# The six buffers of converted weights begin 128 bytes lower in each SBUF partition

## The chip, the cores and the metric

The kernel runs on one core of one Trainium2 chip. The metric is the device time of one execution in microseconds (us). A profile is one execution recorded by the hardware profiler; its engines are PE (TensorE's matmuls), PEld (TensorE's weight loads), DVE (VectorE), ACT (ScalarE), POOL (GpSimd) and SP (the queue that issues most DMAs).

## The reference

One layer of a decoder trunk on 256 tokens of width 2048, all in float32. Shortened to what matters here:

```python
mod = silu(c) @ w_ada + b_ada                     # 2048 -> 6 * 2048: shifts, gains, gates
h = rms_norm(x, norm_mix) * (1 + sc1) + sh1
proj = h @ w_in                                   # 2048 -> three groups of heads
mixed = concat(retention(proj), rwkv7(proj), moba_attention(proj))
x = x + g1 * (mixed @ w_out)                      # 2048 -> 2048
h = rms_norm(x, norm_ffn) * (1 + sc2) + sh2
u = causal_conv3(h @ w_ffn_up) + conv_b           # 2048 -> 2 * 5632
val, gate = split(u)
x = x + g2 * ((silu(gate) * val) @ w_ffn_down)    # 5632 -> 2048
return rms_norm(x, norm_final)
```

The four large products (w_in, w_out, w_ffn_up, w_ffn_down) are nearly all of the arithmetic.

## The kernel before

**How a large product is computed.** Activations lie feature-major: 128 features on the partitions, 256 tokens along the free dimension. A weight matrix comes as blocks of 128 x 128; such a block is the stationary operand of a matmul and a 128 x 256 activation tile is the moving one. For accuracy every value is split in two parts of type fp32r, hi (the rounded value) and lo (what the rounding left), and each block of the product takes three matmuls into one PSUM tile: hi weights with hi activations (line 1192), hi weights with lo activations (1193), lo weights with hi activations (1194). Each of the three loads its own weights, so 3,200 blocks make 9,600 pairs of weight load and matmul. The names of the activation tiles tell the stage: hhi and hlo are the normalised input of w_in and of w_ffn_up, mxhi and mxlo that of w_out, xghi and xglo an early input for the first part of w_ffn_up, ghi and glo the input of w_ffn_down.

**How weights arrive.** SP loads raw weights in tiles of 128 x 2048 float32 (raw). For each half of such a tile `convert_until` (line 448) lets ACT round it into a buffer hi of 8 blocks (line 458) and DVE subtract to get lo (line 459). There are CONVB = 3 buffers hi and 3 buffers lo, used in turn, 4,096 bytes per partition each; block j of a buffer begins 512 j bytes into it. Conversion runs AHEAD = 2 buffers ahead of the matmuls. The order of the instructions on each engine is that in which the Python code issues them; the outer loop (line 1166) takes one converted buffer after another, 8 blocks each, then evacuates finished tiles and runs some steps of the attention-like tasks, whose smaller matmuls lie between those of the large products.

**Where tiles lie.** Pools are laid out one after the other in each partition, and inside a pool in the order of first use: const, arena (30 tiles of 4,096 bytes), stream (three raw buffers of 8,192 bytes, a pad, the three hi, the three lo), small (narrow vectors of the norms, the tile rs_mix / acc / rs_ffn, a pad, more small tiles), and behind them a region that is reused from stage to stage. The start addresses in the built program, per partition:

| tiles | bytes each | first start | start modulo 512 |
|---|---|---|---|
| arena: x, hhi, hlo, mxhi, mxlo, most of ghi and glo, late raw tiles | 4,096 | 31,232 | 0 |
| stream: raw | 8,192 | 154,112 | 0 |
| stream: hi and lo, six buffers | 4,096 | 179,008 | 320 |
| small: narrow vectors of 8 bytes | 8 | 203,584 | 320 to 416 |
| small: rs_mix, acc, rs_ffn | 1,024 | 203,712 | 448 |
| small: xn, nsq | 1,024 | 204,800 | 0 |
| last region, tail: xghi, and the second glo | 4,224 | 207,232 | 384 |
| last region, tail: the first glo | 4,224 | 211,456 | 0 |
| last region, tail: the first ghi | 4,224 | 215,680 | 128 |
| last region, tail: xglo, and the second ghi | 4,224 | 219,904 | 256 |

The tiles inside an activation buffer are 1,024 bytes apart (1,032 for xghi and xglo, which have 258 columns), so the moving operand of nearly all large matmuls begins at a multiple of 512 bytes, and every weight block at 320 modulo 512. The exceptions are the 192 matmuls with xghi and xglo and, in w_ffn_down, the first 24 matmuls of each of the 16 output tiles, which take the tail's ghi and glo. Two pads have a size that the code states: the stream pad at line 348 and SMALL_PAD at line 1061.

Of the kernel before, what the change touches and what calls it, by code (L numbers as in the profile page):

```python
# [8 lines left out]
F32 = mybir.dt.float32  # L9
# [156 lines left out]
WAITS = (7, 20, 28)  # L166
TASKS = 5

CONST_PAD, SMALL_PAD = 32, 16

LEAD = ((116, 0), (145, 8), (152, 6), (164, 4), (172, 3), (186, 1))

# [1 line left out]
def trunk(tc, A):  # L174
# [5 lines left out]
    def pool(name, bufs, **kw):  # L180
        return ctx.enter_context(tc.tile_pool(name=name, bufs=bufs, **kw))
# [3 lines left out]
    stream = pool("stream", 1)  # L185
# [159 lines left out]

    pump()

    stream.tile([128, 80], F32, name="pad")


    silu_c = const.tile([128, 16], F32, name="silu_c")
# [928 lines left out]
```

## Time and profile before

| | |
|---|---|
| median of 3 runs | 1285.11 us (1283.68 to 1285.34) |
| the profiled execution | 1284.61 us, of which the span from first to last instruction is 1282.8 us |
| granted TensorE clock, mean | 0.987 |
| PE busy | 1242.3 us (97%), 10,524 matmuls |
| DVE, ACT, POOL busy | 1031.6 us (80%), 650.6 us (51%), 39.9 us (3%) |
| bytes moved | 320.56 MB, mean 250 GB/s |

Matmuls overlap in the array: each stands in the trace with some 0.28 us although the next one starts about 0.11 us later. So the busy time of PE tells only whether PE ever stood still; how fast a run of matmuls goes is read from the distance between two starts, or from a stretch's length and the number of matmuls in it (two of which had begun before the stretch).

### The profile page before, as it was taken

How to read it: one execution, taken by the hardware profiler on the slowest of the kernel's cores; microseconds unless marked ns; L12 is line 12 of the kernel's file. 1: busy time of each engine (PE TensorE's matmuls, PEld its weight loads, DVE VectorE, ACT ScalarE, POOL GpSimd, SP SyncE). 2: the span in 40 equal slices, each digit the busy share in tenths (PEclk: the TensorE clock that was granted, in tenths of full speed). 3: DMA queues.
4: the chain of work that ended last, by engine and by line, in shares of the span. 5: the costliest groups of instructions: out<-in, count | busy, mean ns of one | idle time of the engine just before them, and what ended most of it. 6: DMA issues, size and time to landing. Idle time of an engine off the chain costs nothing.

```text
span 1282.8 us, 25320 instructions
## 1 busy us (share of the span) xinstructions
PE 1242.3 (97%) x10524; PEld 1222.0 (95%) x10524; DVE 1031.6 (80%) x1606; ACT 650.6 (51%) x1043; POOL 39.9 (3%) x41
## 2 busy tenths in 40 slices
PE   5899999999999999999999999999999999999996
PEld 4799999999998999999999999999999999999995
DVE  7988989989988478999896999899866766666444
ACT  4455444665435333566555656666555544444441
POOL 0000000000000000500000000000000000000000
PEclk7999999999999999999999999999999999999998
DMA  9999987786636459867985566565655677777551
GB/s 388 349 360 344 341 311 268 290 294 209 232 104 235 155 204 363 319 233 259 350 307 200 197 213 208 184 225 194 220 205 198 230 263 254 285 254 281 207 197 66
DMA packets 49939, 320.56 MB, mean 250 GB/s; under 512 B 5536, under 2 KB 6048, under 8 KB 15776
## 3 DMA queue, kind: packets, MB, share of 16 engines
q1 hardware_dynamic: 48528, 315.10, 67.8%
q0 software_dynamic: 1008, 3.67, 0.8%
q8 instruction: 82, 1.34, 0.4%
q14 instruction: 33, 0.27, 0.1%
q10 hardware_dynamic: 288, 0.17, 0.0%
HBM read 316.83 MB, written 2.10 MB: 249 GB/s over the span
## 4 chain that ended last, share of the span: by engine, by line
PE 89%; DVE 7%; issue 2%; ACT 1%; DMA 0%; POOL 0%; DVEq 0%; ACTq 0%; POOLq 0%
PE mm L1192 26%; PE mm L1194 26%; PE mm L1193 26%; DVE raw L413 2%; DVE lo L459 2%; PE pair L1194 1%; PE pair L1192 1%; PE pair L1193 1%; PE xx L778 1%; PE u L915 1%; PE sp L923 1%; PE sp L937 1%; PE akv L788 1%; PE yps L917 0%; ACT hi L458 0%
## 5 line engine op out<-in xcount | busy, mean ns | idle before, releaser
L459 DVE TENSOR_TENSOR lo<-raw,hi 128x1024 fp32r<-128x1024 f32 x400 | 488.4, 1224 | 161.0 <-ACT hi L458 158.2
L458 ACT CAST hi<-raw 128x1024 fp32r<-128x1024 f32 x400 | 418.7, 1049 | 391.7 <-PE mm L1193 333.0
L1192 PE MATMUL mm<-hhi,hi 128*128 128x256 f32 x2016 | 560.2, 278 | 0.2
L1194 PE MATMUL mm<-hhi,lo 128*128 128x256 f32 x2016 | 559.4, 278 | 0.7 <-DVE lo L459 0.7
L1193 PE MATMUL mm<-hlo,hi 128*128 128x256 f32 x2016 | 559.5, 278 | 0.0
L1194 PEld LDWEIGHTS mm<-hhi,lo 128*128 128x128 f32 x2016 | 379.2, 188 | 1.7 <-DVE lo L459 1.3
L1192 PEld LDWEIGHTS mm<-hhi,hi 128*128 128x128 f32 x2016 | 379.1, 188 | 1.3 <-issue 0.3
L1193 PEld LDWEIGHTS mm<-hlo,hi 128*128 128x128 f32 x2016 | 378.8, 188 | 0.3
L413 DVE SCALAR_TENSOR_TENSOR raw<-raw,cb 128x2048 f32<-128x2048 f32 x96 | 221.3, 2305 | 10.4 <-DMA raw<-w_ada 9.6
L1192 PE MATMUL mm<-ghi,hi 128*128 128x256 f32 x704 | 194.8, 277 | 0.0
L1193 PE MATMUL mm<-glo,hi 128*128 128x256 f32 x704 | 194.8, 277 | 0.0
L1194 PE MATMUL mm<-ghi,lo 128*128 128x256 f32 x704 | 194.8, 277 | 0.0
L1192 PEld LDWEIGHTS mm<-ghi,hi 128*128 128x128 f32 x704 | 132.2, 188 | 0.0
L1194 PEld LDWEIGHTS mm<-ghi,lo 128*128 128x128 f32 x704 | 132.2, 188 | 0.0
L1193 PEld LDWEIGHTS mm<-glo,hi 128*128 128x128 f32 x704 | 132.2, 188 | 0.0
L1192 PE MATMUL mm<-mxhi,hi 128*128 128x256 f32 x256 | 73.9, 289 | 1.3 <-DVE x L1032 1.3
L1194 PE MATMUL mm<-mxhi,lo 128*128 128x256 f32 x256 | 72.1, 282 | 0.5 <-DVE lo L459 0.5
L1193 PE MATMUL mm<-mxlo,hi 128*128 128x256 f32 x256 | 72.3, 283 | 0.0
L1046 POOL TENSOR_TENSOR acc<-acc,nsq 128x256 f32<-128x256 f32 x28 | 34.0, 1213 | 808.4 <-ACT nsq L1045 808.2
L1192 PE MATMUL pair<-hhi,hi 128*128 128x256 f32 x160 | 45.0, 294 | 7.6 <-ACT hi L458 5.6
L1192 PEld LDWEIGHTS mm<-mxhi,hi 128*128 128x128 f32 x256 | 48.3, 188 | 3.2 <-DVE x L1032 1.2
L1194 PEld LDWEIGHTS mm<-mxhi,lo 128*128 128x128 f32 x256 | 48.5, 189 | 0.6 <-DVE lo L459 0.6
(292 smaller groups left out, 1301.5 us busy)
## 6 DMA issues: line engine op xcount, KB each, us to landing
raw<-w_ada SPq DMA_DIRECT2D x96, 1024.0 KB, 5.7
raw<-w_up SPq DMA_DIRECT2D x67, 1024.0 KB, 4.8
raw<-w_in SPq DMA_DIRECT2D x52, 1024.0 KB, 6.6
raw<-w_down SPq DMA_DIRECT2D x44, 1024.0 KB, 4.9
raw<-w_up SPq DMA_DIRECT2D x42, 512.0 KB, 8.1
raw<-w_out SPq DMA_DIRECT2D x18, 512.0 KB, 9.1
raw<-w_out SPq DMA_DIRECT2D x7, 1024.0 KB, 5.0
x<-xT SPq DMA_DIRECT2D x4, 512.0 KB, 5.4
```

Of the source, the lines that this page charges most:

```text
L413: V.scalar_tensor_tensor(raw, raw, 1.0, cb, op0=OP.mult, op1=OP.mult, accum_out=m)
L458: S.copy(flat(hi), src)
L459: V.tensor_tensor(flat(lo), src, flat(hi).bitcast(F32), op=OP.subtract)
L778: PE.matmul(ps[:, T * i:T * i + 128], L[pb, f, sl], At[pb, f, sl], start=True, stop=True)
L788: PE.matmul(ps[:, 128 * i + 64 * e:128 * i + 64 * e + 64], xv[:, e, 128 * i:128 * i + 128], vT[:, h, 64 * hd:64 * hd + 64], start=True, st ...
L915: PE.matmul(ups[pb, 128 * f:128 * f + 128], M1[:, f, ts], sb[:, f], start=True, stop=True)
L923: PE.matmul(sp[:, fs], kT[pb, h, fs], vT[pb, h, fs], start=(f == 0), stop=False, skip_group_check=True)
L937: PE.matmul(sp[:, fs], bT[pb, h, fs], U[pb, h, fs], start=False, stop=True, skip_group_check=True)
L1046: (V if t == NF - 1 else G).tensor_tensor(norm["acc"], norm["acc"], sq, op=OP.add)
L1192: PE.matmul(ps, whi[:, j], hi, start=first and not (two and t % 2), stop=False, skip_group_check=two)
L1193: PE.matmul(ps, whi[:, j], lo, start=False, stop=False, skip_group_check=two)
L1194: PE.matmul(ps, wlo[:, j], hi, start=False, stop=last, skip_group_check=two)
```

## The change

Two pads of one column count change, the one by -32 float32 columns (128 bytes), the other by +32.

```diff
-CONST_PAD, SMALL_PAD = 32, 16
+CONST_PAD, SMALL_PAD = 32, 48
...
-    stream.tile([128, 80], F32, name="pad")
+    stream.tile([128, 48], F32, name="pad")
```

By this the six buffers hi and lo begin 128 bytes lower, at 192 modulo 512 in place of 320. The narrow 8-byte vectors and the tile rs_mix / acc / rs_ffn behind them move down with them (the tile from 448 to 320). The larger pad in small takes up the 128 bytes, so xn, nsq and all that follows stay where they were; so do const, arena and the raw buffers. Every instruction on every engine, its order and its waits are the same as before.

## Rows read from the trace of the kernel before

**Rows 1.** The page: engine busy time, and the granted clock in 40 slices
```profile
PE 1242.3 (97%) x10524; PEld 1222.0 (95%) x10524; DVE 1031.6 (80%) x1606; ACT 650.6 (51%) x1043; POOL 39.9 (3%) x41
...
PEclk7999999999999999999999999999999999999998
```

**Rows 2.** The page's costliest groups: out<-in, count, busy us, mean ns
```profile
L1192 PE MATMUL mm<-hhi,hi 128*128 128x256 f32 x2016 | 560.2, 278 | 0.2
...
L1192 PE MATMUL mm<-ghi,hi 128*128 128x256 f32 x704 | 194.8, 277 | 0.0
...
L1192 PE MATMUL mm<-mxhi,hi 128*128 128x256 f32 x256 | 73.9, 289 | 1.3 <-DVE x L1032 1.3
...
L1192 PE MATMUL pair<-hhi,hi 128*128 128x256 f32 x160 | 45.0, 294 | 7.6 <-ACT hi L458 5.6
```

**Rows 3.** Stretches of PE: from:to, length, PE busy (matmuls), granted clock, DMA share, GB/s
```profile
140.00:194.00 54.00, 54.00 (x461) 1.00 0.88 334
216.00:229.00 13.00, 13.00 (x117) 1.00 0.84 313
...
570.00:1027.00 457.00, 457.00 (x4035) 1.00 0.65 226
...
1027.00:1271.00 244.00, 241.78 (x2118) 1.00 0.64 229
```

**Rows 4.** PE in order of time, w_ffn_up: start us, us, instruction
```profile
570.78 0.28 PE L1192 MATMUL mm<-hhi,hi 128*128 128x256 f32 x1
...
571.23 0.28 PE L1193 MATMUL mm<-hlo,hi 128*128 128x256 f32 x1
...
571.68 0.28 PE L1194 MATMUL mm<-hhi,lo 128*128 128x256 f32 x1
```

**Rows 5.** PE in order of time, w_out
```profile
504.77 0.28 PE L1194 MATMUL mm<-mxhi,lo 128*128 128x256 f32 x1
...
505.94 0.28 PE L1192 MATMUL mm<-mxhi,hi 128*128 128x256 f32 x1
```

**Rows 6.** Weight loads in order of time, w_ffn_up
```profile
571.12 0.19 PEld L1193 LDWEIGHTS mm<-hlo,hi 128*128 128x128 f32 x1
571.23 0.19 PEld L1194 LDWEIGHTS mm<-hhi,lo 128*128 128x128 f32 x1
```

**Rows 7.** Groups of PE by shape, 571 to 1026 us
```profile
L1193 PE MATMUL mm<-hlo,hi 128*128 128x256 f32 x1339 | 369.6, 276 | 0.0
```

**Rows 8.** Groups of PE by shape, 502.2 to 534 us
```profile
L1193 PE MATMUL mm<-mxlo,hi 128*128 128x256 f32 x91 | 25.6, 281 | 0.0
```

**Rows 9.** Groups of PE by shape, 80 to 540 us
```profile
L1193 PE MATMUL mm<-hlo,hi 128*128 128x256 f32 x613 | 172.2, 281 | 0.0
...
L1193 PE MATMUL mm<-mxlo,hi 128*128 128x256 f32 x247 | 69.8, 283 | 0.0
```

**Rows 10.** PE in order of time, first k-blocks of one tile of w_ffn_down
```profile
1042.12 0.28 PE L1192 MATMUL mm<-ghi,hi 128*128 128x256 f32 x1
...
1043.52 0.28 PE L1192 MATMUL mm<-ghi,hi 128*128 128x256 f32 x1
...
1044.93 0.28 PE L1192 MATMUL mm<-ghi,hi 128*128 128x256 f32 x1
```

**Rows 11.** Groups of PE by shape, 541 to 570 us
```profile
L1192 PE MATMUL mm<-xghi,hi 128*128 128x258 f32 x64 | 18.2, 285 | 0.0
L1193 PE MATMUL mm<-xglo,hi 128*128 128x258 f32 x64 | 18.0, 282 | 0.0
```

**Rows 12.** Groups of DVE by shape, whole span
```profile
L459 DVE TENSOR_TENSOR lo<-raw,hi 128x1024 fp32r<-128x1024 f32 x400 | 488.4, 1224 | 161.0 <-ACT hi L458 158.2 <-PE mm L1194 1.0 <-DMA raw<-w_out 0.5
...
L439 DVE SCALAR_TENSOR_TENSOR xn<-x,mod_mix_gain,rs_mix 128x256 f32<-128x256 f32 x16 | 7.7, 484 | 0.5
...
L1086 DVE TENSOR_TENSOR up<-up,rs_ffn 128x1024 f32<-128x1024 f32 x4 | 4.8, 1221 | 0.0
```

**Rows 13.** Groups of ACT by shape, whole span
```profile
L458 ACT CAST hi<-raw 128x1024 fp32r<-128x1024 f32 x400 | 418.7, 1049 | 391.7 <-PE mm L1193 333.0 <-issue 15.2 <-PE pair L1193 13.4
...
L363 ACT ACTIVATE sq<-x 128x1024 f32<-128x1024 f32 x4 | 4.2, 1054 | 0.3 <-DMA x<-xT 0.3
```

## The prediction

> **What bounds the kernel now.** I read the page's busy line first. PE is busy 97% of the span, and the clock line stands at 9 tenths or more except at the two ends, where it is 7 and 8 [rows 1], so the kernel is a chain of matmuls at the high clock level (2.4 GHz), and what counts is how far apart two of them start. The stretches show where: from 570 to 1027 us PE is busy 457.00 of 457.00 us, from 1027 to 1271 us 241.78 of 244.00 [rows 3]. In these 701 us no other engine holds PE up to speak of, and each nanosecond per matmul is a nanosecond of the time.
>
> Then I looked at the spacing itself, and it has two values for the same instruction. From 570 to 1027 us, 4,035 matmuls less the two already under way make 457.00 / 4,033 = 113.3 ns each [rows 3]; start by start, 8 steps from 570.78 to 571.68 are 0.90 us [rows 4]. In w_out, 10 steps from 504.77 to 505.94 take 1.17 us, 117 ns [rows 5]. Inside w_in both occur: 54.00 / 459 = 117.6 ns from 140 to 194 us and 13.00 / 115 = 113.0 ns from 216 to 229 us, at the same granted clock of 1.00 and a similar DMA share (0.88 and 0.84) [rows 3]. So neither clock, nor load on the DMA engines, nor shape tells them apart; each holds for hundreds of matmuls once it is entered. I call them the short spacing (113.3) and the long one (117.6, the value of the longest such stretch). The mean duration of a group shows which it runs at: 276 ns at the short spacing, 281 at the long [rows 7, 8], in either case about 163 ns more than the spacing.
>
> What the trace offers as a cause is placement. A matmul streams its moving tile while the next matmul's weights are loaded: the load of the next block starts within 0.01 us of the running matmul, and that block's matmul 0.11 us after it [rows 4, 6]. Both read SBUF. Where the moving tile doesn't begin at a multiple of 512 bytes, the short spacing is lost: the first 24 matmuls of each tile of w_ffn_down take ghi and glo at 128, 0, 256 and 384 modulo 512, and 24 steps from 1042.12 to 1044.93 are 2.81 us, 117.1 ns [rows 10], between two stretches of aligned tiles that run at the short one (ghi as a whole, mostly aligned, has 277 ns [rows 2]). The xghi and xglo matmuls, at 256 to 408 modulo 512, have 282 to 285 ns [rows 11], so about 120 ns apart. So the distance between the two reads seems to matter, and the change alters this distance for all 9,600 large matmuls.
>
> **The change part by part.** No instruction, wait or DMA is added, removed or moved. What changes are three kinds of addresses.
>
> *The hi and lo buffers as weights.* Write D for moving start minus weight start, modulo 512. Before, an aligned moving tile has D = 0 - 320 = 192, the D under which 113.3 is held for 4,033 matmuls. After, it has D = 0 - 192 = 320. The rows of before have this D in one place: tiles at 128, whose D was 128 - 320 = 320 too. They are the first ghi of w_ffn_down, and the 12 steps in which they stand, mixed 2 to 1 with aligned glo tiles, go from 1042.12 to 1043.52, 1.40 us, 116.7 ns [rows 10]. That is the nearest evidence, and it is the long spacing. A lower bound: D = 320 by itself costs nothing, and the rows at 128 are slow because D changes from one matmul to the next; then up and down keep 113.3. An upper bound: the 120 ns of the xghi tiles. I take 117.6, 4.3 ns over the short spacing, because rows 10 are the only ones with this D and the spacing is one in which the kernel demonstrably stays.
>
> How many matmuls are at the short spacing now? In w_ffn_up 4,033 x 4.3 ns = 17.3 us. In w_ffn_down 2,118 - 16 x 24 = 1,734 x 4.3 = 7.5 us. Before 541 us there are 3 x 613 + 3 x 247 = 2,580 matmuls in the two groups shown, at mean durations of 281 and 283 ns [rows 9], which says that most are at the long spacing already; the means also hold some much longer ones, so I count a third as short, an estimate: 860 x 4.3 = 3.7 us. The 576 matmuls with tiles off a multiple of 512 get another D as well; they are at 117 to 120 now and I leave them there, give or take 4 ns, 2.3 us either way. Sum: 17.3 + 7.5 + 3.7 = 28.5 us.
>
> *The same buffers as targets of ACT and DVE.* ACT's rounding takes 1,049 ns at 320 modulo 512, and an ACT operation of the same size wholly on aligned tiles takes 1,054 [rows 13]. DVE's subtraction takes 1,224 ns, and a multiplication of the same size on aligned tiles 1,221 [rows 12]. So placement doesn't show in either engine, within 0.5%. If 192 did cost one of them 5%, 400 x 61 ns = 24 us on DVE, it would lie beside PE: DVE is idle a fifth of the span [rows 1], and ACT's waits before the rounding are 333.0 us for matmuls to give buffers free [rows 13].
>
> *The narrow vectors and rs_mix.* 16 operations read rs_mix at 484 ns [rows 12] and 16 rs_ffn alike. A tenth more or less would be 32 x 48 ns = 1.5 us of DVE, hidden by the same idle time. I cost them at nothing. If PE slows, loads and conversions only get more time, so nothing else becomes late.
>
> Against the profiled execution: 1284.6 + 28.5 = 1313.1 us, rounded to 1313. That execution is 0.5 us under the median of the runs, less than these estimates can resolve.
>
> A rule speaks against all this. The Trainium skill, page "SBUF — State Buffer", section "Who interferes with whom", says that PE never waits for anyone at SBUF, and the page "TensorE: Matmul & The Clock Gate" (Part 2, step-by-step) that loading the next weights takes no read bandwidth from the running matmul, since PE has two independent read ports. By that rule addresses would mean nothing and the sum would be 0. The trace disagrees as far as two spacings of one instruction can tell, 113.3 and 117.6 ns in rows 3.
>
> **The rivals.**
>
> *No change.* The two spacings come from how the matmuls were last interrupted, and rows 10 are slow only because D varies. Then the long runs settle at 113.3 as before, and the time is 1285 within about 2.6 us. For it: both spacings exist at one D in w_in. Against it: the loss sets in at once wherever a moving tile is off the multiple, in every tile of w_ffn_down.
>
> *Faster: the early stretches fall to the short spacing.* The place is w_in and w_out. If D = 320 holds 113.3 more firmly than 192, the two thirds of 2,580 now at the long one gain 1,720 x 4.3 = 7.4 us, and up to 2.3 us come from the off-multiple tiles: 1275 us. It decides if after every interruption the matmuls come back at 0.113 us. For it: before 541 us the kernel is mostly at the long spacing, so there is something to gain. Against it: rows 10.
>
> *Faster: 113.3 isn't the floor.* If it holds a collision of the two reads, another D may remove it. The Trainium skill's page "TensorE: Matmul & The Clock Gate", section "Back-to-back issue gap", gives N / 2.4 + 2.5 ns, by estimate 109.2 ns for 256 columns. From the rows alone, a 4 ns gain like the step between the two spacings would be 9,600 x 4 = 38 us: 1246 us. Against it: in no group is the mean under 276 ns, whichever of the four offsets its tiles have [rows 2, 7, 11].
>
> *Slower still.* At D = 320 the matmuls run like those of xghi, about 120 ns less a nanosecond for their two extra columns, 119.7: 6.4 x (4,033 + 1,734 + 860) = 42 us and 2.1 x 1,720 = 4 us more: 1330 us. It decides if a stretch of w_ffn_up shows 283 ns or more.
>
> **How the numbers follow.** The forecast (long spacing through w_ffn_up and w_ffn_down, 1305 to 1320) gets 0.42. Only some of the stretches going long, 1290 to 1305, gets 0.06, slower still 0.13. That makes slower 0.61. No change within 0.2% (2.6 us, about what a measurement of this kernel can tell) gets 0.16. Faster gets 0.23, of which 0.20 is the early stretches and 0.03 the lower floor. The range takes in the 1275 of the first and the 1330 of the heavy case, since cases of both signs have weight: 1275 to 1331. It leaves out the lower floor and the outer halves of these two cases, together under 0.2. The likeliest case's own range is 1303 to 1322.
>
> **What would show it.** Right: between about 570 and 1050 us, starts 0.117 to 0.118 us apart and a mean duration near 281 ns for hhi, hi; w_ffn_up some 17 us longer; DVE and ACT durations as before; DVE and ACT idle longer. The rival of no change shows 276 ns there. The early gain shows in w_in and w_out: 276 in place of 281 to 283. Wrong altogether: a mean under 276 ns, or a time that moves with PE's spacing unchanged, by DVE or ACT operations that take another time at their new addresses.

## The result and the profile after

The changed kernel takes 1295.70 us (median of 4 runs, 1293.31 to 1296.36), the kernel before 1284.59 us in the same comparison: a ratio of 1.0092, 95% interval 1.0074 to 1.0111. It is slower, as forecast, by 11 us where 28.5 were forecast. Of all 57 timed executions of the kernel before, here and beside the experiments, 8 took 1304 to 1310 us at the granted clock of the others (0.986 to 0.990); none of them was recorded, so what they ran at is not known, and the ratios leave them out.

The page after, answering to [rows 1]:

```profile
span 1294.5 us, 25320 instructions
...
PE 1254.7 (97%) x10524; PEld 1234.8 (95%) x10524; DVE 1032.9 (80%) x1606; ACT 650.4 (50%) x1043; POOL 40.0 (3%) x41
```

The span grew by 11.7 us and PE's busy time by 12.4; DVE and ACT worked as long as before. So the time lies in PE. The stretches of the changed kernel (columns as in [rows 3]):

```profile
140.00:194.00 54.00, 54.00 (x460) 1.00 0.88 330
216.00:229.00 13.00, 13.00 (x112) 1.00 0.82 290
575.00:1030.00 455.00, 455.00 (x4017) 1.00 0.64 227
1032.00:1280.00 248.00, 247.84 (x2105) 1.00 0.62 225
```

Less the two matmuls under way at the start of each, these are 117.9 and 118.2 ns per matmul in w_in (the second was 113.0), 113.3 in w_ffn_up as before, and 117.9 in w_ffn_down, where [rows 3] give 244.00 / 2,116 = 115.3, or 114.3 without the 2.2 us in which PE stands idle at the end. So one stage that ran at the short spacing kept it and another lost it, at one and the same placement. The mean durations say the same; w_ffn_up, answering to [rows 7]:

```profile
L1193 PE MATMUL mm<-hlo,hi 128*128 128x256 f32 x1339 | 369.6, 276 | 0.0
```

and w_ffn_down, 1032 to 1280 us, whose group had 277 ns over the whole kernel before [rows 2]:

```profile
L1193 PE MATMUL mm<-glo,hi 128*128 128x256 f32 x702 | 196.4, 280 | 0.0
```

The first matmul of w_ffn_up behind the xghi tiles and the first of w_ffn_down, in order of time, fix the account:

```profile
574.02 0.28 PE L1192 MATMUL mm<-hhi,hi 128*128 128x256 f32 x1
...
1030.98 0.28 PE L1192 MATMUL mm<-ghi,hi 128*128 128x256 f32 x1
```

The same two before:

```profile
570.09 0.28 PE L1192 MATMUL mm<-hhi,hi 128*128 128x256 f32 x1
...
1027.06 0.28 PE L1192 MATMUL mm<-ghi,hi 128*128 128x256 f32 x1
```

So 3.9 us come from all that lies ahead of w_ffn_up, none from w_ffn_up (457.0 us in both), and 7.8 from w_ffn_down and the end: 11.7 us, the whole growth of the span.

Not all of the 3.9 us is spacing. The same 315 matmuls, between the same two instructions, took 40.0 us before and 41.9 after, at a lower granted clock:

```profile
422.00:462.00 40.00, 40.00 (x315) 0.96 0.31 109
```

```profile
424.04:465.94 41.90, 41.90 (x315) 0.92 0.30 103
```

That is 1.9 us, which leaves 2.0 for the spacing and all else. The same 315 matmuls in two later executions of the changed placement, whose kernels are alike up to there (E13, then E14):

```profile
421.68:460.46 38.78, 38.78 (x315) 1.00 0.33 112
```

```profile
425.94:466.29 40.35, 40.35 (x315) 0.96 0.31 107
```

So the granted clock of this stretch differs from one execution to the next, and the time with it.

DVE and ACT at the new addresses, answering to [rows 12, 13]:

```profile
L459 DVE TENSOR_TENSOR lo<-raw,hi 128x1024 fp32r<-128x1024 f32 x400 | 488.6, 1224 | 170.5 <-ACT hi L458 169.1
L439 DVE SCALAR_TENSOR_TENSOR xn<-x,mod_mix_gain,rs_mix 128x256 f32<-128x256 f32 x16 | 7.7, 484 | 0.5
```

```profile
L458 ACT CAST hi<-raw 128x1024 fp32r<-128x1024 f32 x400 | 418.5, 1048 | 405.8 <-PE mm L1193 339.4 <-issue 15.2 <-PE pair L1193 13.2
```

1,224, 484 and 1,048 ns, against 1,224, 484 and 1,049: the move of 128 bytes is nothing to either engine.

### The profile page after: what moved, and what is told of

Its sections match the earlier page's. It is cut to its first block, busy times and chain, and to the rows that moved or that the text cites. A ratio compares the mean times of both kernels' runs of the same rounds, so it can differ in the third digit from the quotient of the medians.

```text
span 1294.5 us, 25320 instructions
## 1 busy us (share of the span) xinstructions
PE 1254.7 (97%) x10524; PEld 1234.8 (95%) x10524; DVE 1032.9 (80%) x1606; ACT 650.4 (50%) x1043; POOL 40.0 (3%) x41
## 4 chain that ended last, share of the span: by engine, by line
PE 89%; DVE 8%; issue 1%; DMA 1%; ACT 1%; POOL 0%; DVEq 0%; ACTq 0%; POOLq 0%
PE mm L1192 26%; PE mm L1193 26%; PE mm L1194 26%; DVE raw L413 2%; DVE lo L459 2%; PE pair L1192 1%; PE pair L1194 1%; PE pair L1193 1%; PE xx L778 1%; PE u L915 1%; PE sp L923 1%; ACT hi L458 1%; PE sp L937 1%; DMA raw<-w_ada 1%; PE akv L788 1%
## 5 line engine op out<-in xcount | busy, mean ns | idle before, releaser
L459 DVE TENSOR_TENSOR lo<-raw,hi 128x1024 fp32r<-128x1024 f32 x400 | 488.6, 1224 | 170.5 <-ACT hi L458 169.1
L458 ACT CAST hi<-raw 128x1024 fp32r<-128x1024 f32 x400 | 418.5, 1048 | 405.8 <-PE mm L1193 339.4
```

The lines of the kernel that those rows point to most:

```text
L458: S.copy(flat(hi), src)
L459: V.tensor_tensor(flat(lo), src, flat(hi).bitcast(F32), op=OP.subtract)
```

## The experiments

Each was timed beside the kernel before on one chip; the ratio is to the kernel before there. One execution of each was recorded, and the stretches are from that one. Where stretches are shown, the columns are those of [rows 3], and a spacing is the length over the matmuls less two. The two-valued spacing is the question throughout: what decides which value a stretch gets?

**E1, one extra matmul in w_ffn_up of the changed kernel.**

```diff
+    def kick():
+        y = ybank("kick")
+        PE.matmul(y[:, 0:128], ident, ident, start=True, stop=True)
+
+    hooks.setdefault(first_up + 24, []).append(kick)
```

> One small extra matmul (128 columns, its result unused) is put into w_ffn_up of the changed kernel, some 24 converted buffers after the stage begins, near 605 us; nothing else changes. Theory A (entry): at this placement both spacings, 113.3 and 117.8 ns, are steady, and a run of matmuls keeps the one it fell into when it began; in the changed kernel every run that began after an interruption is at 117.8, and only w_ffn_up, which began out of the xghi tiles, is at 113.3. Then the matmuls behind the extra one run at 117.8: some 3,720 x 4.4 ns, 16 us, about 1312 us, and the mean duration from 620 to 1020 us is 279 to 281 ns. Theory B (stage): something in w_ffn_up itself holds 113.3 (its tile order, its operands). Then the spacing is back at 113.3 within a few matmuls and the time is 0.5 us over the changed kernel's, about 1296 us, 276 ns.

Measured: 1311.59 us, ratio 1.0224 (1.0208 to 1.0240). PE in order of time at the extra matmul, then the stretches before and behind it:

```profile
615.94 0.28 PE L1200 MATMUL mm<-hhi,lo 128*128 128x256 f32 x1
616.06 0.38 PE L1168 MATMUL kick<-cst 128*128 128x128 f32 x2
616.20 0.37 PE L1198 MATMUL mm<-hhi,hi 128*128 128x256 f32 x1
616.40 0.28 PE L1199 MATMUL mm<-hlo,hi 128*128 128x256 f32 x1
```

```profile
574.00:614.00 40.00, 40.00 (x355) 1.00 0.72 254
620.00:1030.00 410.00, 410.00 (x3483) 1.00 0.62 214
```

113.3 ns before, 117.8 behind. The extra matmul (two records in the trace) holds the stream up by about 0.23 us: the start at 616.40 would have been at 616.17. It costs 16 us, since the 3,650 matmuls behind it never return to the short spacing. Theory A holds and B falls: nothing in w_ffn_up keeps it at 113.3.

**E2, the same extra matmul in the kernel before.**

> The same extra matmul at the same place in the kernel before. Theory A: both spacings are steady here too, and after an interruption about a third to a half of the runs before 541 us were short; so the rest of w_ffn_up is either all short (about 1285 us, 276 ns) or all long (about 1301 us, 281 ns), with nothing between but by a later interruption. Theory B: 1285 us, 276 ns.

Measured: 1283.54 us, ratio 1.0012 (0.9998 to 1.0025), no difference clear of the noise. A stretch of w_in and the one behind the extra matmul:

```profile
140.00:194.00 54.00, 54.00 (x476) 1.00 0.89 341
...
620.00:1020.00 400.00, 400.00 (x3532) 1.00 0.64 221
```

Behind it the spacing is 113.3 again, which both theories allow here. What tells more is w_in: 54.00 / 474 = 113.9 ns where the kernel before, with the same instructions and addresses at this point, had 117.6 [rows 3]. So the same stretch can get either value from one execution to the next. At the changed placement it does so too: E1's execution, identical there, has the first of these two rows, and the changed kernel's the second.

```profile
140.00:194.00 54.00, 54.00 (x476) 1.00 0.90 341
```

```profile
140.00:194.00 54.00, 54.00 (x460) 1.00 0.88 330
```

**E5, the six buffers alone.** (The edit is shown against the changed kernel: SMALL_PAD goes back to its old value, and a 128-byte tile behind the six buffers keeps the room.)

```diff
-CONST_PAD, SMALL_PAD = 32, 48
+CONST_PAD, SMALL_PAD = 32, 16
...
+        if c == 0:
+            stream.tile([128, 32], F32, name="pad2")
```

> Only the six buffers move by 128 bytes; the narrow vectors and rs_mix / acc / rs_ffn stay where they were (their room is kept by a 128-byte tile behind the six buffers). If the spacing of the matmuls is the whole matter: the changed kernel's time within 0.2%, ratio 1.007 to 1.011, w_ffn_up at 276 ns and w_ffn_down at 279 to 280. If the narrow tiles had a part in it: a ratio nearer to 1.

Measured: 1295.29 us, ratio 1.0116 (1.0058 to 1.0174).

```profile
600.00:1000.00 400.00, 400.00 (x3532) 1.00 0.66 227
1070.00:1260.00 190.00, 190.00 (x1616) 1.00 0.67 238
```

113.3 ns in w_ffn_up, 117.7 in w_ffn_down: the changed kernel's picture without the narrow tiles. No part of theirs is seen. The interval is wide because one of the four times was 1306.23 us.

**E3, E4, E6, E7, E8, E12: other starts of the six buffers**, all by the same edit, here that of E3:

```diff
-CONST_PAD, SMALL_PAD = 32, 16
+CONST_PAD, SMALL_PAD = 32, 80
...
-    stream.tile([128, 80], F32, name="pad")
+    stream.tile([128, 16], F32, name="pad")
```

Start 64: 

> The six buffers at 64 modulo 512 (stream pad 16, SMALL_PAD 80), so the distance D of moving start minus weight start is 448 for aligned tiles. Theory A: again the same two spacings and no third; each long stretch is wholly at 113.3 or wholly at 117.8, and the time lies between 1277 us (all short) and 1314 us (all long). Rival theory C (each distance has its own stall): a spacing of its own, such as 115 or 120 ns, in all stretches alike, and a time in proportion: 1300 us at 115, 1345 us at 120.

Start 0: 

> The six buffers at 0 modulo 512 (no stream pad, SMALL_PAD 96): weights and aligned moving tiles begin at the same place modulo 512, D = 0. Theory A: the same two spacings, 1277 to 1314 us. Theory C: at equal starts the two reads meet most; one spacing in all stretches, 118 ns or more, 1320 us or more.

Start 128: 

> The six buffers at 128 modulo 512, D = 384. So far the buffers at 64, 192 and 320, all 64 beyond a multiple of 128, have the two spacings 113.3 and 117.8, and the buffers at 0 have 120.0 throughout. Theory D1 (start modulo 128): every multiple of 128 does as 0 does: 120 ns in all stretches, about 1331 us. Theory D2 (distance): only where weights and moving tile start together do the reads meet so often; at 128 the two spacings are back, 1277 to 1314 us.

Start 256: 

> The six buffers at 256 modulo 512, D = 256. Theory D1: 120 ns, about 1331 us. Theory D2: 1277 to 1314 us. A third way (period 256): as at 0 here, 1331 us, but not at 128 and 384.

Start 384: 

> The six buffers at 384 modulo 512, D = 128. Theory D1: 120 ns, about 1331 us. Theory D2: 1277 to 1314 us. Period 256: as at 128.

Start 96: 

> The six buffers at 96 modulo 512 (stream pad 24, SMALL_PAD 72). What is known: starts 0 and 256 give 120.0 ns, 128 and 384 give 118.7 on average, 64 and 320 mostly 113.3, 192 both. If the loss falls off with the distance from the multiples of 128: between 64 and 128, either the two spacings as at 64 (1277 to 1314 us) or a single one between 113.3 and 118.7, at its middle about 1300 us. A better placement than 64 would show 276 ns in w_in and w_out too, about 1277 us.

Measured (medians), with the spacing of w_ffn_up from 600 to 1000 us and of w_ffn_down from 1070 to 1260:

| start modulo 512 | start modulo 256 | us | ratio (95%) | w_ffn_up, ns | w_ffn_down, ns |
|---|---|---|---|---|---|
| 320 (before) | 64 | 1284.59 | 1 | 113.3 | 114.0 |
| 64 (E3) | 64 | 1282.40 | 0.9991 (0.9976 to 1.0005) | 113.3 | 114.0 |
| 192 (changed) | 192 | 1295.70 | 1.0092 (1.0074 to 1.0111) | 113.3 | 117.8 |
| 96 (E12) | 96 | 1322.19 | 1.0292 (1.0274 to 1.0310) | 118.7 | 119.5 |
| 128 (E6) | 128 | 1319.55 | 1.0301 (1.0261 to 1.0341) | 118.6 | 118.5 |
| 384 (E8) | 128 | 1318.73 | 1.0299 (1.0251 to 1.0347) | 118.7 | 118.5 |
| 0 (E4) | 0 | 1330.87 | 1.0371 (1.0355 to 1.0388) | 120.0 | 119.6 |
| 256 (E7) | 0 | 1329.25 | 1.0367 (1.0334 to 1.0400) | 120.0 | 119.6 |

The rows of E4 behind it, then those of w_ffn_up in E7 (start 256), E6 (128), E12 (96) and E3 (64):

```profile
600.00:1000.00 400.00, 400.00 (x3336) 1.00 0.62 215
1070.00:1260.00 190.00, 190.00 (x1591) 1.00 0.71 251
```

```profile
600.00:1000.00 400.00, 400.00 (x3336) 1.00 0.62 216
```

```profile
600.00:1000.00 400.00, 400.00 (x3374) 1.00 0.63 218
```

```profile
600.00:1000.00 400.00, 400.00 (x3373) 1.00 0.62 218
```

```profile
600.00:1000.00 400.00, 400.00 (x3532) 1.00 0.65 227
```

Starts that agree modulo 256 give the same time, though they differ modulo 512: 64 and 320, 128 and 384, 0 and 256. So D1 (all multiples of 128 alike at 120.0) and D2 (only equal starts collide) both fall, and the third way, period 256, was right but for 128, which has a mean of its own. Theory C, which I had set against A, holds as well: at 0, 96 and 128 the distance gives long stretches their own mean spacing, and of the starts tried only those 64 beyond a multiple of 128 have the short one. A is no law for every placement; it describes these. The forecast for 96 missed: it is as slow as 128, 1322 us where at most 1314 was expected, so the loss doesn't fall off with the distance from the multiples of 128.

**E11, everything 64 bytes lower, the distance kept.**

```diff
-CONST_PAD, SMALL_PAD = 32, 16
+CONST_PAD, SMALL_PAD = 16, 16
```

> The kernel before with CONST_PAD 16 in place of 32: all tiles behind const begin 64 bytes lower, moving tiles at 448 modulo 512 and the six buffers at 256, the start at which the kernel had 120.0 ns with moving tiles at 0. The distance is as before, 192. If the distance alone decides: the two spacings of the kernel before, w_ffn_up at 276 ns, 1277 to 1314 us and most likely 1284. If the start of the weights itself decides: 120 ns, about 1330 us. If a moving tile off 512 costs by itself: 117 ns or more throughout, 1313 us or more.

Measured: 1283.63 us, ratio 0.9985 (0.9970 to 1.0000).

```profile
600.00:1000.00 400.00, 400.00 (x3532) 1.00 0.64 226
1070.00:1260.00 190.00, 190.00 (x1668) 1.00 0.63 227
```

With the weights at 256, where E7 had 120.0 ns, and the moving tiles at 448, w_ffn_up is at 113.3. Neither address alone decides between the two times; their distance does. (That rests on this one shift.)

**E9 and E10, the tail's tiles at multiples of 512**, in the changed kernel and in that of E3. The core of the edit (in E9; 4 buffers u in place of 5 make room):

```diff
-        return tail[0].tile([128, 1056], F32R, tag="gt", name=name)
+        wide = name[0] == "x" or len(GT) == 1
+        return tail[0].tile([128, 1152 if wide else 1024], F32R, tag="xg" if wide else "gt", name=name, bufs=2)
...
+        tail[0].tile([128, 32], F32, name="pad3", bufs=1)
```

E9: 

> The changed kernel, with the tail's tiles xghi, xglo and the four early ghi and glo moved to multiples of 512 (a 128-byte pad, two sizes of buffer, and 4 buffers u in place of 5 to make room), so w_ffn_down has no tile off the multiple. Theory A (entry): w_ffn_down then begins straight out of w_ffn_up and keeps the spacing that w_ffn_up ends with, whichever it is, through all 16 tiles. If w_ffn_up is short: w_ffn_down at 276 ns, 7.5 us less than the changed kernel, about 1288 us; if w_ffn_up became long (its entry changes too, since xghi and xglo move): both long, about 1313 us. Theory B (stage): w_ffn_down is long at this placement whatever precedes it: w_ffn_up 276 ns, w_ffn_down 279 to 280, about 1295 us.

E10: 

> The six buffers at 64 modulo 512 and the tail aligned as well. Theory A: both spacings; at 64 most runs before 541 us were short. All short from 570 us on would be about 1280 us, since the 384 matmuls of w_ffn_down off the multiple gain 3.8 ns each, 1.5 us, and the 192 of xghi and xglo up to 6 ns each, 1.2 us. If the new entry into w_ffn_up makes it long: about 1306 us.

Measured: E9 1310.70 us, ratio 1.0199 (1.0181 to 1.0217); E10 1283.07 us, 0.9982 (0.9970 to 0.9994). E9, then E10:

```profile
600.00:1000.00 400.00, 400.00 (x3399) 1.00 0.62 220
1070.00:1260.00 190.00, 190.00 (x1615) 1.00 0.68 245
```

```profile
600.00:1000.00 400.00, 400.00 (x3532) 1.00 0.64 227
1070.00:1260.00 190.00, 190.00 (x1679) 1.00 0.64 233
```

Without tiles off the multiple both stages share one spacing, 117.8 and 117.8 in E9, 113.3 and 113.3 in E10. E9 can't tell A from B, since its w_ffn_up, entered out of other xghi addresses, was long already. E10 is the only version below the kernel before by more than its interval, by 0.2%; against E3 the two ratios differ by 1 us, inside their intervals, where 2.7 were expected.

**E13, only the early ghi and glo aligned** in the changed kernel; xghi and xglo keep 384 and 256, and with them the entry into w_ffn_up.

```diff
+        if name[0] == "x" or len(GT) == 1:
+            one = name in ("xghi",) or name[:3] == "ghi"
+            n, at = (1056, 32) if one else (1088, 64)
+            x = tail[0].tile([128, n], F32R, tag="xa" if one else "xb", name=name, bufs=1)
...
+            return x if name[0] == "x" else x[:, at:]
+        return tail[0].tile([128, 1024], F32R, tag="gt", name=name, bufs=2)
```

> The changed kernel with the four early ghi and glo tiles at multiples of 512; xghi and xglo stay at 384 and 256, so that the entry into w_ffn_up is the changed kernel's (4 buffers u in place of 5 make room). Theory A (entry): w_ffn_up short as in the changed kernel, and w_ffn_down, with nothing off the multiple in its way, keeps it: 276 ns in both, 7.5 + 1.5 us less than the changed kernel, about 1287 us. Theory B (stage): w_ffn_down long at this placement whatever precedes it, 279 to 280 ns, about 1294 us.

Measured in the profiled execution, 1282.94 us:

```profile
600.00:1000.00 400.00, 400.00 (x3532) 1.00 0.64 227
1070.00:1260.00 190.00, 190.00 (x1679) 1.00 0.65 233
```

113.3 ns in both: w_ffn_down keeps the short spacing at the changed placement once nothing off the multiple stands in its way. Theory A holds in this execution, and B, by which it must be long, falls. The four times are 1282.94, 1285.48, 1306.59 and 1313.91 us, so no ratio is given. Only the first was recorded. What the two long ones ran at is not shown; the kernel before took 1304 to 1307 us in 3 of 8 times beside them.

**E14, E13 with an extra matmul in the middle of w_ffn_down** (the edit of E1, at first_down + 44).

> The same with one small extra matmul in the middle of w_ffn_down (half of its 88 converted buffers). Theory A: short up to it and, as after nearly all interruptions at this placement, long behind it: 276 ns before about 1147 us and 279 to 280 ns after, 1,050 x 4.4 ns, 4.7 us more than without it. Theory B: no difference before and behind it, 0.5 us more.

Measured: the recorded execution takes 1292.33 us, the three others 1307.61 to 1313.99, and the ratio, 1.0153 (1.0060 to 1.0245), can't resolve the 4.7 us that were forecast. The stretches and the extra matmul of the recorded one:

```profile
600.00:1000.00 400.00, 400.00 (x3532) 1.00 0.64 227
1060.00:1145.00 85.00, 85.00 (x753) 1.00 0.75 271
1155.00:1260.00 105.00, 105.00 (x894) 1.00 0.60 211
```

```profile
1151.10 0.38 PE L1175 MATMUL kick<-cst 128*128 128x128 f32 x2
```

113.3, then 113.2 up to the extra matmul, and 117.7 behind it. w_ffn_down falls from the one spacing to the other by a single interruption, as w_ffn_up did in E1. From its first start to its last it takes 244.2 us, in E13's execution 239.3: 4.9 us more, close to the forecast.

## Why the prediction was wrong

*That PE's spacing is the whole matter* was right: DVE and ACT took as long as before, and E5 gives the same picture without the narrow tiles. One term was missing from it, the granted clock, which differed between the two recorded executions in one stretch (0.96 and 0.92) and goes with 1.9 us of their 11.7.

*That the distance between moving tile and weights decides* was right in kind: E11 keeps the distance and keeps the time, and in the table only the start of the six buffers and of the narrow tiles differs. For the three pairs tried the period is 256 bytes rather than the 512 that I worked with. That a moving tile off a multiple of 512 loses the short spacing was a wrong reading of [rows 10]: in E11 nearly all of them are off it, at 448, and run at 113.3 ns.

*The failed step* is "I take 117.6" for every aligned matmul at D = 320, and with it the 17.3 us of w_ffn_up. I had seen that the two spacings both occur at D = 192 and that each holds once entered, and then gave D = 320 one spacing. It has both as well. The rows that I leaned on, [rows 10], could not tell: there the distance modulo 256 changes between 64 and 192 within the three matmuls of each block. w_ffn_up came out of the xghi tiles at the short one and kept it, 0 us in place of 17.3. E1 shows that the spacing depends on how the run was entered and is no property of the stage, for the last 3,650 of these matmuls ran at 117.8 after one extra matmul.

*w_ffn_down*, 7.5 us forecast: 7.8 measured with the end, but for a reason that the working didn't give, so the agreement is luck. It is long since each of its tiles begins with 24 matmuls off the multiple, out of which this placement comes back long (E13 takes them away, and its recorded execution is short), while the one before comes back short, 114.0 ns in the table.

*The stages before 541 us*, 3.7 us forecast: w_ffn_up began 3.9 us later, and this agreement is luck too. 1.9 us of it came at the lower granted clock, and some 2 us are left for spacing, as in the stretch from 216 to 229 us, 113.0 to 118.2 ns. How often the long one is entered there is not fixed: the stretch from 140 to 194 us went either way at both placements (E2), and w_ffn_up begins at 570.06 us in E13's execution and at 574.46 in E14's, though the two kernels are the same up to there.

*The rivals.* No change was right for w_ffn_up alone, and for its reason, that the spacing depends on how the run was last interrupted. Faster in the early stages did not come. A lower floor: in none of the placements is a long stretch under 113.3 ns. The 120 ns of the heavy case exist, at starts 0 and 256 and not at 192. By the rule of the Trainium skill ("SBUF — State Buffer", "Who interferes with whom") PE waits for nobody at SBUF. If that made addresses indifferent, the runs disagree: E7 and E11, both with weights at 256, differ in addresses alone and by 6.7 ns per matmul. No run shows whether it is PE's two reads that meet.

What stays open: what in SBUF or in PE makes the spacing depend on the distance, and what in the moment of entry picks the spacing. No run here shows either.

## What to carry to other kernels

Where a stream of matmuls loads new weights for each, read its spacing from a long undisturbed stretch and try the start of the weight buffers relative to the moving tiles in steps of 64 bytes; here the kernel before and the worst start differ by 3.7%. If the spacing has two steady values, look for what the stream last stumbled over before pricing a stage at either: one small matmul in the wrong place cost 16 us. A sum over stages must ask for each how it is entered, not only what it runs at elsewhere.

## What the runs showed of the hardware that I had not expected

- The spacing of matmuls with 256 moving columns and a new weight load each depends on the distance of the two SBUF addresses, in the starts tried modulo 256 bytes: 113.3 or 117.8 ns at 64 and 192, 118.5 to 118.7 at 128, 119.6 to 120.0 at 0 (E1, E3 to E8, E11).
- At distances of 64 and 192 two spacings are steady. The 6,144 matmuls of w_ffn_up and w_ffn_down held 113.3 in E13, and 3,650 held 117.8 behind the extra matmul in E1, both at 64; at 192 the kernel before held 117.6 for 459 matmuls of w_in and 113.3 for 4,033 of w_ffn_up.
- The same instructions at the same addresses take either one in different executions (w_in from 140 to 194 us, 117.6 ns in the kernel before and 113.9 in E2, whose only difference comes later).
